# Hybrid diffusion step on one Trainium2 core: where two groups of modulation weights are issued, and how the prologue is ordered

## The chip, the core and the metric

The kernel runs on one core of a Trainium2 chip. The metric is the device time of one execution in microseconds. Engines are named as the profile names them: PE is TensorE (matrix products, with PEld its weight loads), DVE is VectorE, ACT is ScalarE, POOL is GpSimd, and SP is the engine that issues most of the DMA transfers.

## The reference

Two layers (DEPTH = 2, width D = 1024) are applied to 128 context tokens and 512 latent tokens, 640 tokens in all. Each layer has three parallel mixers on one input projection (a two-directional RWKV-7 scan, differential attention, a Hyena long convolution), an output projection and an MLP. Three parts matter here.

Modulation: a vector of 6 x 1024 numbers per token group and layer, which gives shift, scale and gate of the mixer and of the MLP:

```python
mod_ctx = (jax.nn.silu(c_ctx) @ w_mod[l] + b_mod[l])[None, None, :]
...
sh1, sc1, gt1, sh2, sc2, gt2 = jnp.split(mod, 6, axis=-1)
h = _rmsnorm(x, p['g_mix_pre']) * (1.0 + sc1) + sh1
...
x = x + gt1 * _rmsnorm(mix, p['g_mix_post'])
h = _rmsnorm(x, p['g_ffn_pre']) * (1.0 + sc2) + sh2
...
x = x + gt2 * _rmsnorm(f, p['g_ffn_post'])
```

Hyena filters: a small sine network of the position, whose last weight gives two directions per order, normalised and transformed:

```python
h = (h @ p['hy_w3']).reshape(L, HY_ORDER, HY_DIRS, D_C)
h = h * jnp.exp(-t[:, :, None, None] * jnp.abs(p['hy_decay']))
h_fwd, h_bwd = h[:, :, 0], h[:, :, 1]
filt = jnp.concatenate([h_fwd, zeros, h_bwd[:0:-1]], axis=0)
filt = filt * lax.rsqrt(jnp.sum(filt * filt, axis=0, keepdims=True) + 1e-6)
return jnp.fft.rfft(filt, axis=0)
```

RWKV decay and rate, which go through small weights of rank 64 and then through tanh or sigmoid, per direction `d`:

```python
wl = -jax.nn.softplus(-(p['rwkv_w0'][d] + jnp.tanh(uw[d]) @ p['rwkv_w2'][d])) - 0.5
a = jax.nn.sigmoid(p['rwkv_a0'][d] + ua[d] @ p['rwkv_a2'][d])
```

## The kernel before

Tokens are five tiles of 128 (four latent, one context). Feature-major activations are 128 x 640 tiles. Float32 products of large weights are written as three products of a high and a low part, which a helper (`split`, lines 143 to 149) makes from the raw tile. Raw weight tiles of 512 KB go through one pool of three buffers (`wr`), which the modulation weights share.

The stages of the program follow each other: a prologue (modulation group 0 of layer 0, filter networks and filter spectra of both layers, normalisation of the tokens into `act`), and then for each layer the Hyena columns and long convolution with the RWKV columns (`hyena_rwkv_columns`), the operand stage (`rw_operands` with the q/k/v projections of `qkv_columns`), attention, the scan (`rw_scan`), the output projection, and the MLP.

The order of work is written by Python generators. In the operand stage, `rw_operands` is stepped, and on every fifth step one q or k projection is issued. In the scan, `weave` steps about a dozen actors in rounds (inversions, state updates, finishes), and after each round the generator `back` once. `back` is the modulation: one step of `mod_group` (line 275) issues one load of 512 KB on SP's queue and two products of a 128 x 32 weight (the conditioning) with 512 columns of it into one bank, `psmod` (line 293). A group has 16 such steps, then an add of the bias (line 298), for two of three groups a product with gains, four transposes into columns (`pscol`), small copies, and stores of rows. Group 0 (shift and scale of the mixer) is needed at the layer's beginning, group 1 (gate of the mixer, shift of the MLP) and group 2 (scale and gate of the MLP) after the output projection. `mods_late` yields groups 1 and 2, and then, in the first layer, group 0 of the next one; all 48 (first layer) or 32 steps (second) run in the scan.

A planner with a simulated timeline then orders each engine's queue: among instructions that are ready it prefers those that were written first. `issue_after` ties a block's instructions behind a given one of the same engine.

PSUM has eight banks: in the layer's first part two belong to `b1`, four to `b2` (two tiles of two banks) and two to `hz` (one tile of two banks). `hz` serves the transforms of the convolution, and in the operand stage the products of the decay and rate weights (`mm640`, line 585: two halves of 320 columns into the two banks), which one ScalarE instruction of 640 columns reads with its tanh (lines 929 and 933).

In the prologue, `filter_nets` computes the sine networks of both layers, then the rest of the modulation steps and then the loads of the five token tiles (`xl`) are written; `norm_tok` scales each token by its own norm (line 1423) and `norm_feat` transposes, applies group 0's scale and shift, and splits. `hyena_consts` loads the transform's constants on GpSimd's queue after the third token tile. `filter_spectra` makes, for each layer and order, five tiles of both directions, `hft` (line 1215), their squares for the norm, their sum and difference `hpm` (line 1239, ten 128 x 256 instructions), the high and low parts of these, and the transforms.

Of the kernel before, what the change touches and what calls it, by code (L numbers as in the profile page):

```python
# [111 lines left out]
class Net:  # L112
# [47 lines left out]
    def phz(self, nm="hz"):  # L160
        return self.t(self.hz, [P, 2, 512], F32, "hz", nm)

# [193 lines left out]
    def mods_late(self, l, pool, out):  # L356
        rs = []
        yield from self.mod_group(l, 1, pool, rs)
        d1 = self.mod_rows(rs[0], (0, 1))
        S2 = self.mod_shift(self.mod_cols(rs[0])(2), "S2")  # L360
        yield
        yield from self.mod_group(l, 2, pool, rs)
        G2 = self.mod_scale(self.mod_cols(rs[1])(0), V_GFP, "G2", self.vecs[l])
        d2 = self.mod_rows(rs[1], (2, 3))
        out += [d1, S2, G2, d2]
        yield
        if l + 1 < self.nl:
            yield from self.mods(l + 1, pool)
# [552 lines left out]
    def rw_prep(self, l, p, d, w, tw, ua, w2, a2, smask, S, pair, pool, psm):  # L921
# [11 lines left out]
        nc.scalar.activation(self.h2(aa), self.mm640(a2[ds_, fs], ua[ds_]), AF.Tanh, scale=0.5,  # L933
                             bias=self.hb[:, 4 + 2 * d + p:5 + 2 * d + p])
# [46 lines left out]
        for e in range(2):  # L981
# [5 lines left out]
                "pmid": pmid, "pend": pend}  # L987

# [163 lines left out]
    def filter_loads(self, tp, setup, between):  # L1152
# [5 lines left out]
        for l in range(self.nl):  # L1158
            nc.sync.dma_start(self.vecs[l], I["vec"][l])
            hw1 = self.t(tp, [33, 64], F32, "hw1")  # L1160
            nc.sync.dma_start(hw1, I["hy_w1"][l])
            next(between)
            hw2 = self.t(tp, [64, 64], F32, "hw2")
            nc.sync.dma_start(hw2, I["hy_w2"][l])
            out.append({"w": (hw1, hw2), "h": emb})
        next(setup)
        for l, f in enumerate(out):
            hw3 = f["w3"] = self.t(tp, [P, 1024], F32, "hw3")
            nc.gpsimd.memset(hw3[64:], 0.0)
            nc.sync.dma_start(hw3[:64], I["hy_w3"][l])  # L1170
            next(between)
            dec = f["dec"] = self.t(tp, [P, 256], F32, "hdec")
            nc.sync.dma_start(dec, I["hdec"][l])
        return out

    def filter_nets(self, nets, tp):

        nc = self.nc
        for i, b in enumerate((V_B1, V_B2)):
            for l, f in enumerate(nets):  # L1180
                vec = self.vecs[l]
# [20 lines left out]
    def filter_spectra(self, l, f, tp):  # L1202
# [4 lines left out]
        for o in range(2):  # L1207
            fts = []
            acc = None
            for i in range(NT):  # L1210
                ps = self.pb1("psh")
                nc.tensor.matmul(ps, f["h"][:, i * P:(i + 1) * P], f["w3"][:, o * 512:o * 512 + 512],
                                 start=True, stop=True)
# [5 lines left out]
                fts.append(ft)  # L1219
# [7 lines left out]
                if i in (3, 4):  # L1227
# [6 lines left out]
                    nc.vector.tensor_scalar(out=m[:, cc:cc + 2], in0=psn[:, :2], scalar1=1e-6, scalar2=None, op0=ALU.add)  # L1234
            for cs, op in enumerate((ALU.add, ALU.subtract)):
                spl = []
                for i, ft in enumerate(fts):
                    s = self.t(tp, [P, 256], F32, "hpm")
                    nc.vector.tensor_tensor(out=s, in0=ft[:, 0], in1=ft[:, 1], op=op)
                    hh = self.t(tp, [P, 256], F32R, "hph", bufs=10)  # L1240
                    hl = self.t(tp, [P, 256], F32R, "hpl", bufs=10)
                    self.split(hh, hl, s, "a", "v" if i % 2 else "g")
                    spl.append((hh, hl))
                F = self.t(tp, [P, 2, 512], F32, "hF", bufs=1)
                eo = self.phz("psf")
                for par in range(2):
                    tb = self.dftf[par, cs]
                    for ft_ in range(2):
                        for kt in range(2):
                            a = (tb[:, 0, kt, ft_ * P:(ft_ + 1) * P], tb[:, 1, kt, ft_ * P:(ft_ + 1) * P])  # L1250
                            self.mm3(eo[:, par, ft_ * 256:ft_ * 256 + 256], a, spl[par * 2 + kt], kt == 0, kt == 1)
# [9 lines left out]
                self.mm3(ps[:, :256], (self.dftc[:, cs, 0], self.dftc[:, cs, 1]), spl[4], True, True)  # L1261
# [204 lines left out]
    def prologue(self, xsrc, setup):  # L1466
        nc = self.nc
        with ExitStack() as c:
# [7 lines left out]
            self.filter_nets(nets, ph)  # L1476
            for _ in mods:
                pass
            act = self.act_tiles()
            xn = []  # L1480
            for j in range(NT):
# [4 lines left out]
                if j == 2:  # L1486
                    with self.tc.issue_after(self.last_rstd):
                        self.hyena_consts(ph)
                if j == 2:
                    self.norm_feat(xn, 0, 3, self.G1, self.S1, act, pn, True)  # L1490
# [38 lines left out]
    def qkv_columns(self, l, act, pv):  # L1529
# [14 lines left out]
        pss = [x[:, 0], x[:, 1], y[:, 0], y[:, 1], self.phz("psB1")[:, 0]]  # L1544
# [9 lines left out]
    def layer(self, l, act, xsrc, xdst):  # L1554
# [227 lines left out]
```

## Time and profile before

| | us |
|---|---|
| median of 3 runs (lowest, highest) | 2269.79 (2259.91, 2269.84) |
| the profiled execution, its own time | 2268.23 |
| its span, first to last instruction | 2266.5 |
| TensorE busy | 2129.4 |
| VectorE busy | 1458.9 |
| ScalarE busy | 824.1 |
| GpSimd busy | 799.8 |
| mean granted TensorE clock | 0.974 of full |

Busy time of an engine is the union of its instructions' records; matmuls are pipelined, and a busy TensorE is not one at its peak. The granted clock is that of TensorE, as a share of 2.4 GHz; it has two levels, 1.2 and 2.4 GHz, and a value between is the mean over a stretch. DMA share is the mean busy share of the 16 DMA engines. A name such as `psmod<-wr,sc` is output and inputs of an instruction by the program's names, and L293 the line of the kernel. Groups by stretch ("windows") give, for a piece of the span in us, each engine's busy time and in parentheses its instructions.

### The profile page before, as it was taken

The numbers are of one execution on the slowest core, as the hardware profiler recorded it, in microseconds if no ns is written. First come the engines' busy times: TensorE is split into PE (matmuls) and PEld (weight loads), VectorE is DVE, ScalarE is ACT, GpSimd is POOL, SyncE is SP. The second block draws the span as 40 slices with busy tenths as digits, with TensorE's granted clock in tenths as the row PEclk, the third lists the DMA queues.
The fourth block names the chain that finished last, engine by engine and source line by source line (L and its number), as shares of the span: only waits on it lengthen the run. The fifth ranks groups of instructions, "written<-read, shape, count | busy, mean of one in ns | idle before, by whom it ended". The sixth has DMA issues, their size and how long they took to land. (4 is left out here: it accounts for less than half of the span.)

```text
span 2266.5 us, 33997 instructions
## 1 busy us (share of the span) xinstructions
PE 2129.4 (94%) x13236; PEld 1806.3 (80%) x13236; DVE 1458.9 (64%) x2188; ACT 824.1 (36%) x1644; POOL 799.8 (35%) x781
## 2 busy tenths in 40 slices
PE   7899997899999899999999999889999989999998
PEld 2799985666687799898988999656688878989896
DVE  6776658865575764655666575886576584637475
ACT  4442232653342533222324223265344352313131
POOL 3434434541012424342522443464112232524251
PEclk8899998999999899999999999999999999999999
DMA  8244431135405222222254333223510512222233
GB/s 305 77 139 158 132 100 63 57 124 195 162 3 182 75 84 72 87 75 86 76 173 174 105 121 103 72 77 105 196 39 26 205 47 93 76 75 87 81 105 118
DMA packets 86071, 245.42 MB, mean 108 GB/s; under 512 B 12196, under 2 KB 24996, under 8 KB 85909
## 3 DMA queue, kind: packets, MB, share of 16 engines
q1 hardware_dynamic: 80148, 222.34, 29.1%
q0 software_dynamic: 5760, 20.91, 3.0%
q8 instruction: 104, 1.70, 0.3%
q14 instruction: 59, 0.48, 0.1%
HBM read 214.80 MB, written 28.87 MB: 108 GB/s over the span
## 5 line engine op out<-in xcount | busy, mean ns | idle before, releaser
L388 PE MATMUL psA<-act,wh 128*128 128x320 f32 x1472 | 304.2, 319 | 1.1 <-ACT uhr L1503 0.5
L388 PEld LDWEIGHTS psA<-act,wh 128*128 128x128 f32 x1472 | 238.0, 192 | 11.3 <-issue 8.6
L176 PE MATMUL psB<-wl,f 128*128 128x512 f32 x560 | 218.4, 390 | 0.9 <-POOL wl L143 0.9
L177 PE MATMUL psB<-wh,f 128*128 128x512 f32 x560 | 218.4, 390 | 0.0
L143 POOL TENSOR_TENSOR wl<-wr,wh 128x1024 fp32r<-128x1024 f32 x42 | 103.4, 2461 | 304.2 <-DVE wh L149 136.7
L175 PE MATMUL psB<-wh,f 128*128 128x512 f32 x560 | 209.4, 390 | 0.0
L388 PE MATMUL psA<-act,wl 128*128 128x320 f32 x736 | 180.3, 316 | 0.8 <-DVE wl L143 0.8
L143 DVE TENSOR_TENSOR wl<-wr,wh 128x1024 fp32r<-128x1024 f32 x84 | 105.2, 1252 | 63.2 <-ACT wh L147 61.7
L457 POOL TENSOR_TENSOR fft<-ffb 128x512 f32<-128x512 f32 x56 | 89.7, 1601 | 128.3 <-DMA ffb<-in_w_ff_dram 55.4
L388 PEld LDWEIGHTS psA<-act,wl 128*128 128x128 f32 x736 | 127.1, 192 | 3.5 <-issue 2.1
L147 ACT CAST wh<-wr 128x1024 fp32r<-128x1024 f32 x63 | 66.1, 1049 | 168.4 <-PE psB L177 85.6
L176 PEld LDWEIGHTS psB<-wl,f 128*128 128x128 f32 x560 | 105.2, 188 | 22.8 <-POOL wl L143 1.3
L177 PEld LDWEIGHTS psB<-wh,f 128*128 128x128 f32 x560 | 105.2, 188 | 21.8
L175 PEld LDWEIGHTS psB<-wh,f 128*128 128x128 f32 x560 | 105.2, 188 | 21.6
L149 DVE CAST wh<-wr 128x1024 fp32r<-128x1024 f32 x63 | 51.1, 812 | 91.8 <-PE psB L177 63.5
L1054 DVE TENSOR_TENSOR x<-b,cmask 128x512 f16<-128x512 f32 x120 | 80.4, 686 | 33.5 <-PE b L1053 33.2
L147 ACT CAST f<-ffr 128x640 fp32r<-128x640 f32 x64 | 43.8, 726 | 154.3 <-DVE ffr L497 154.3
L1063 ACT CAST t<-px 128x512 f16<-128x512 f32 x100 | 58.7, 588 | 102.0 <-PE px L1058 100.8
L505 DVE TENSOR_TENSOR ffr<-ffr,psF 128x320 f32<-128x320 f32 x140 | 67.4, 482 | 37.2 <-POOL ffr L505 20.6
L505 POOL TENSOR_TENSOR ffr<-ffr 128x320 f32<-128x320 f32 x56 | 54.8, 978 | 95.8 <-DVE ffr L505 84.8
L1025 PE MATMUL b<-ZR,bp 128*128 128x256 f32 x320 | 85.5, 392 | 1.6 <-DVE x L1054 0.8
L177 PE MATMUL psF<-ffS,wl 128*128 128x320 f32 x256 | 80.4, 314 | 5.2 <-DVE wl L143 5.2
(461 smaller groups left out, 6038.1 us busy)
## 6 DMA issues: line engine op xcount, KB each, us to landing
wr<-in_w_mod_dram SPq DMA_DIRECT2D x83, 512.0 KB
wr<-in_w_ff_dram SPq DMA_DIRECT2D x72, 512.0 KB
wr<-in_w_in_dram SPq DMA_DIRECT2D x46, 512.0 KB
x<-x SPq DMA_DIRECT2D x30, 512.0 KB
ffa<-in_w_ff_dram SPq DMA_DIRECT2D x28, 512.0 KB
ffb<-in_w_ff_dram SPq DMA_DIRECT2D x28, 512.0 KB
dft<-in_k_dftf_dram POOLq DMA_DIRECT2D x16, 512.0 KB, 6.7
dft<-in_k_dfti_dram POOLq DMA_DIRECT2D x16, 512.0 KB, 4.9
```

The source lines that it names most:

```text
L143: eng.tensor_tensor(out=l, in0=src, in1=h.bitcast(F32), op=ALU.subtract)
L147: self.nc.scalar.copy(out, in_)
L149: self.nc.vector.tensor_copy(out, in_)
L175: nc.tensor.matmul(out, a[0], b[0], start=first, stop=False)
L176: nc.tensor.matmul(out, a[0], b[1], start=False, stop=False)
L177: nc.tensor.matmul(out, a[1], b[0], start=False, stop=last)
L388: self.nc.tensor.matmul(ps[:, hf, :320], (h, l)[a][:, k * P:(k + 1) * P], act[b][k][:, hf * 320:hf * 320 + 320], start=k == 0 and i == 0, ...
L457: sub = lambda o, x, y: nc.gpsimd.tensor_tensor(out=o, in0=x, in1=y, op=ALU.subtract)
L505: add = lambda o, a, b, e=nc.vector, op=ALU.add: e.tensor_tensor(out=o, in0=a, in1=b, op=op)
L1025: nc.tensor.matmul(ps[:, 2 * e:2 * e + 2], bp[:, q, e], s["ZR"][:, :, j], start=True, stop=True)
L1054: nc.vector.tensor_tensor(out=vw(x16), in0=vw(ps), in1=cm(i), op=ALU.mult)
L1063: nc.scalar.copy(t16, ps1)
```

## The change

Five edits, in the order of the code of a run:

- In the prologue, eleven modulation steps are issued with the five token tiles among them (from the third step of these on, one on every second), each tile loaded and scaled by its own norm. Only then come the filter networks of layer 0, the rest of the modulation and `norm_feat`. The constants of the transform and the filter networks of layer 1 come after `norm_feat`.
- The two filter directions are added and subtracted on the last weight of the network, 64 rows, by GpSimd, so `hft` holds sum and difference at once. The `hpm` instructions go, and splits take 512 columns instead of 256. At the first tap, where the backward direction counts as zero, half of the sum of both parts is written to both. The norm is halved to match. `hft` has two buffers instead of six.
- The operand stage opens PSUM pools of its own: `b2` as before, and in place of the two-bank `hz` one bank `h1` and one bank `pm`.
- The products of the decay and rate weights are read in halves of 320 columns, each through the one bank `h1` (`tanh640`).
- `mods_late` (groups 1 and 2) is stepped in the operand stage, once per step of `rw_operands`, before attention. The scan steps only group 0 of the next layer, and in the last layer nothing.

```diff
@@ mods_late
         out += [d1, S2, G2, d2]
         yield
-        if l + 1 < self.nl:
-            yield from self.mods(l + 1, pool)
@@ rw_prep
-        nc.scalar.activation(self.h2(sw), self.mm640(w2[ds_, fs], tw[ds_]), AF.Tanh, scale=0.5,
-                             bias=self.hb[:, 2 * d + p:2 * d + p + 1])
+        self.tanh640(sw, w2[ds_, fs], tw[ds_], 2 * d + p)
...
+    def tanh640(self, out, lhsT, rhs, i):
+        for hf in range(2):
+            sl = slice(hf * 320, hf * 320 + 320)
+            ps = self.ph1("ps640")[:, :320]
+            self.nc.tensor.matmul(ps, lhsT, rhs[:, sl], start=True, stop=True)
+            self.nc.scalar.activation(out[:, sl], ps, AF.Tanh, scale=0.5, bias=self.hb[:, i:i + 1])
@@ filter_loads
+            w3 = f["w3"] = self.t(tp, [P, 2, 512], F32, "hws")
+            nc.gpsimd.memset(w3[64:], 0.0)
+            for q, op in enumerate((ALU.add, ALU.subtract)):
+                nc.gpsimd.tensor_tensor(out=w3[:64, :, q * 256:q * 256 + 256], in0=hw3[:64, :, :256], in1=hw3[:64, :, 256:],
+                                        op=op)
@@ filter_spectra
-                ft = self.t(tp, [P, 2, 256], F32, "hft", bufs=6)
+                ft = self.t(tp, [P, 2, 256], F32, "hft", bufs=2)
...
                 if i in (0, 4):
-                    nc.vector.memset(ft[0:1, 1], 0.0)
+                    tap = self.t(tp, [1, 1, 256], F32, "htap", bufs=1)
+                    nc.vector.tensor_tensor(out=tap, in0=ft[0:1, 0:1], in1=ft[0:1, 1:2], op=ALU.add)
+                    nc.vector.tensor_scalar(out=ft[0:1], in0=tap.to_broadcast([1, 2, 256]), scalar1=0.5, scalar2=None,
+                                            op0=ALU.mult)
...
-            for cs, op in enumerate((ALU.add, ALU.subtract)):
-                spl = []
-                for i, ft in enumerate(fts):
-                    s = self.t(tp, [P, 256], F32, "hpm")
-                    nc.vector.tensor_tensor(out=s, in0=ft[:, 0], in1=ft[:, 1], op=op)
-                    hh = self.t(tp, [P, 256], F32R, "hph", bufs=10)
-                    hl = self.t(tp, [P, 256], F32R, "hpl", bufs=10)
-                    self.split(hh, hl, s, "a", "v" if i % 2 else "g")
-                    spl.append((hh, hl))
+                hh = self.t(tp, [P, 2, 256], F32R, "hph", bufs=6)
+                hl = self.t(tp, [P, 2, 256], F32R, "hpl", bufs=6)
+                self.split(hh, hl, ft, "a", "v" if i % 2 else "g")
+                spl.append((hh, hl))
+            for cs in range(2):
+                sp = [(x[:, cs], y[:, cs]) for x, y in spl]
@@ prologue
-            self.filter_nets(nets, ph)
-            for _ in mods:
-                pass
-            act = self.act_tiles()
             xn = []
-            for j in range(NT):
+
+            def tokens(j):
                 x = self.t(px, [P, D], F32, "xl")
                 nc.sync.dma_start(x, xsrc[j])
                 self.norm_tok(x, x, pn, self.t(px, [P, D], F16, "xj", bufs=1))
                 xn.append(x)
...
+            for n in range(11):
+                next(mods)
+                if n >= 2 and n % 2 == 0:
+                    tokens(n // 2 - 1)
+            self.filter_nets(nets[:1], ph)
+            for _ in mods:
+                pass
+            act = self.act_tiles()
+            self.norm_feat(xn, 0, 3, self.G1, self.S1, act, pn, True)
             self.norm_feat(xn, 3, 5, self.G1, self.S1, act, pn, True)
             with self.tc.issue_after(self.last_rstd):
+                self.hyena_consts(ph)
                 next(setup)
+            self.filter_nets(nets[1:], ph)
@@ layer
-            self.psum(c1, b2=2, hz=1)
             with ExitStack() as ch:
+                self.psum(ch, b2=2, hz=1)
                 ur = self.hyena_rwkv_columns(l, act, pR, self.sb(ch, "hx", 1), ch)
+            self.psum(c1, b2=2, h1=1, pm=1)
+            self.pmtag = "pm"
...
+            back = self.mods_late(l, self.pS, late)
             next(cols)
             for n, _ in enumerate(self.rw_operands(l, ur, (pk, prw), (ptmp, psm))):
                 if n % 5 == 4:
                     next(cols, None)
+                next(back, None)
+            for _ in back:
+                pass
...
-            self.rw_scan(l, prs, prg, self.sb(c, "rf", 1), self.mods_late(l, self.pS, late))
+            self.rw_scan(l, prs, prg, self.sb(c, "rf", 1), iter(()) if last else self.mods(l + 1, self.pS))
```

## Rows read from the trace of the kernel before

**Rows 1.** Page, part 1: busy us, share of the span, instructions.
```profile
PE 2129.4 (94%) x13236; PEld 1806.3 (80%) x13236; DVE 1458.9 (64%) x2188; ACT 824.1 (36%) x1644; POOL 799.8 (35%) x781
```

**Rows 2.** Stretches, prologue: length, busy us (instructions) by engine, granted clock, DMA share, GB/s.
```profile
30.00:40.00 10.00, 6.87 (x37) 3.01 (x38) 7.33 (x10) 6.56 (x14) 6.80 (x9) 0.86 1.03 406
40.00:90.00 50.00, 38.25 (x169) 29.09 (x170) 38.25 (x80) 27.81 (x61) 20.34 (x27) 0.69 0.42 141
```

**Rows 3.** Timeline, TensorE: start us, length us, engine, line, operation, operands, count.
```profile
41.67 1.06 PE L170 MATMUL pscol<-ident,mrow 128*128 128x128 f32 x4
...
85.68 1.52 PE L388 MATMUL psA<-act,wh 128*128 128x320 f32 x2
```

**Rows 4.** Stretches, all engines: operand stages and scans of both layers.
```profile
283.00:388.80 105.80, 90.91 (x475) 76.17 (x474) 74.56 (x92) 31.51 (x54) 40.36 (x28) 0.90 0.23 72
...
487.60:692.00 204.40, 198.92 (x1736) 142.21 (x1736) 122.44 (x241) 79.57 (x170) 35.65 (x39) 0.99 0.41 135
...
1370.00:1472.50 102.50, 93.81 (x522) 80.76 (x520) 74.25 (x93) 31.80 (x54) 42.77 (x32) 0.95 0.25 82
...
1569.80:1756.00 186.20, 181.54 (x1669) 138.09 (x1669) 118.60 (x234) 79.76 (x170) 37.55 (x39) 1.00 0.31 102
```

**Rows 5.** Stretches, tails of both operand stages.
```profile
360.00:370.00 10.00, 2.19 (x6) 1.34 (x6) 9.96 (x11) 0.00 (x0) 3.30 (x3) 0.57 0.19 52
370.00:380.00 10.00, 8.71 (x25) 6.34 (x24) 9.50 (x12) 0.85 (x2) 5.53 (x3) 0.57 0.01 2
1445.00:1455.00 10.00, 3.23 (x15) 2.24 (x14) 10.00 (x13) 0.37 (x1) 4.90 (x4) 0.77 0.09 23
1455.00:1465.00 10.00, 9.32 (x31) 7.41 (x32) 9.96 (x13) 0.00 (x0) 5.51 (x3) 0.72 0.10 30
```

**Rows 6.** Stretches, modulation products and adds alone (columns PE, PEld, DVE), both scans.
```profile
487.60:692.00 204.40, 45.73 (x192) 6.77 (x192) 2.07 (x3) 0.99 0.41 135
1569.80:1756.00 186.20, 31.39 (x128) 4.45 (x128) 1.38 (x2) 1.00 0.31 102
```

**Rows 7.** Stretches, second scan: early, and after modulation has ended.
```profile
1570.00:1603.00 33.00, 32.59 (x250) 16.62 (x249) 16.74 (x26) 14.15 (x31) 6.47 (x10) 1.00 0.77 255
1660.00:1700.00 40.00, 40.00 (x418) 36.37 (x415) 30.55 (x62) 20.43 (x43) 7.85 (x7) 1.00 0.01 3
```

**Rows 8.** Stretch, modulation products alone, second scan, early.
```profile
1570.00:1603.00 33.00, 15.67 (x64) 2.18 (x64) 0.00 (x0) 1.00 0.77 255
```

**Rows 9.** Timeline, second scan, all engines.
```profile
1576.88 0.39 PE L1053 MATMUL b<-t,m 128*128 128x128 f16 x4
...
1577.20 1.05 PE L293 MATMUL psmod<-wr,sc 128*32 128x512 f32 x4
...
1577.31 0.69 DVE L1054 TENSOR_TENSOR x<-b,cmask 128x512 f16<-128x512 f32 x1 [0.48 <-PE b L1053]
...
1578.18 0.40 PE L1058 MATMUL px<-x,tt 128*128 128x128 f16 x4
...
1578.42 0.39 PE L1060 MATMUL px<-tt,x 128*128 128x128 f16 x4
```

**Rows 10.** Tile sw, ScalarE's read of a tanh product: ns min/median/max.
```profile
L929 ACT ACTIVATE sw<-ps,hb x4: 786/794/797, 297.3 to 336.7; 128x640 f32<-128x640 f32 x4
```

**Rows 11.** Timeline, VectorE, prologue.
```profile
38.25 0.68 DVE L298 TENSOR_TENSOR mrow<-psmod,mbias 128x512 f32<-128x512 f32 x1
...
57.44 1.88 DVE L1423 TENSOR_SCALAR xl<-xl,rstd 128x1024 f32<-128x1024 f32 x2
```

**Rows 12.** VectorE by group, 0 to 86 us: busy us, mean ns, idle before.
```profile
L1239 DVE TENSOR_TENSOR hpm<-hft 128x256 f32<-128x256 f32 x14 | 8.5, 621 | 0.3
...
L143 DVE TENSOR_TENSOR hpl<-hpm,hph 128x256 fp32r<-128x256 f32 x6 | 5.0, 842 | 1.4 <-ACT hph L147 1.4
...
L1184 DVE TENSOR_SCALAR ha<-ps,vec 64x640 f32<-64x640 f32 x4 | 3.7, 930 | 1.0 <-PE ps L585 1.0
...
L1147 DVE SCALAR_TENSOR_TENSOR ha<-hq,ha 64x640 f32<-64x640 f32 x4 | 3.3, 816 | 0.1
```

More of the change, by code (lines that the diff above doesn't have):

```diff
@@ L161, in phz, with ph1 @@
         return self.t(self.hz, [P, 2, 512], F32, "hz", nm)
+    def ph1(self, nm="h1"):
+        return self.t(self.h1, [P, 512], F32, "h1", nm)
     def pb1(self, nm="b1"):
@@ L928, in rw_prep @@
         sw, aa = S("sw"), S("aa")
-        nc.scalar.activation(self.h2(sw), self.mm640(w2[ds_, fs], tw[ds_]), AF.Tanh, scale=0.5,
-                             bias=self.hb[:, 2 * d + p:2 * d + p + 1])
+        self.tanh640(sw, w2[ds_, fs], tw[ds_], 2 * d + p)
         yield
         nc.vector.tensor_scalar(out=sw, in0=sw, scalar1=0.5, scalar2=0.5, op0=ALU.mult, op1=ALU.add)
-        nc.scalar.activation(self.h2(aa), self.mm640(a2[ds_, fs], ua[ds_]), AF.Tanh, scale=0.5,
-                             bias=self.hb[:, 4 + 2 * d + p:5 + 2 * d + p])
+        self.tanh640(aa, a2[ds_, fs], ua[ds_], 4 + 2 * d + p)
         yield
@@ L1164, in filter_loads @@
             nc.sync.dma_start(hw2, I["hy_w2"][l])
-            out.append({"w": (hw1, hw2), "h": emb})
+            out.append({"l": l, "w": (hw1, hw2), "h": emb})
         next(setup)
         for l, f in enumerate(out):
-            hw3 = f["w3"] = self.t(tp, [P, 1024], F32, "hw3")
+            hw3 = self.t(tp, [P, 2, 512], F32, "hw3", bufs=1)
             nc.gpsimd.memset(hw3[64:], 0.0)
-            nc.sync.dma_start(hw3[:64], I["hy_w3"][l])
+            nc.sync.dma_start(hw3[:64], I["hy_w3"][l].rearrange("p (o c) -> p o c", o=2))
             next(between)
+            w3 = f["w3"] = self.t(tp, [P, 2, 512], F32, "hws")
[3 more added lines that the diff above has]
+                                        op=op)
             dec = f["dec"] = self.t(tp, [P, 256], F32, "hdec")
@@ L1179, in filter_nets @@
         for i, b in enumerate((V_B1, V_B2)):
-            for l, f in enumerate(nets):
-                vec = self.vecs[l]
+            for f in nets:
+                vec = self.vecs[f["l"]]
                 ps = self.mm640(f["w"][i], f["h"], 64)
@@ L1207, in filter_spectra @@
         for o in range(2):
-            fts = []
+            spl = []
             acc = None
@@ L1211, in filter_spectra @@
                 ps = self.pb1("psh")
-                nc.tensor.matmul(ps, f["h"][:, i * P:(i + 1) * P], f["w3"][:, o * 512:o * 512 + 512],
-                                 start=True, stop=True)
-                ft = self.t(tp, [P, 2, 256], F32, "hft", bufs=6)
+                nc.tensor.matmul(ps, f["h"][:, i * P:(i + 1) * P], f["w3"][:, o], start=True, stop=True)
+                ft = self.t(tp, [P, 2, 256], F32, "hft", bufs=2)
                 nc.vector.tensor_tensor(out=ft, in0=ps.rearrange("p (d c) -> p d c", d=2),
@@ L1233, in filter_spectra @@
                     cc = (i == 4) * 4 + o * 2
-                    nc.vector.tensor_scalar(out=m[:, cc:cc + 2], in0=psn[:, :2], scalar1=1e-6, scalar2=None, op0=ALU.add)
-            for cs, op in enumerate((ALU.add, ALU.subtract)):
-                spl = []
-                for i, ft in enumerate(fts):
-                    s = self.t(tp, [P, 256], F32, "hpm")
-                    nc.vector.tensor_tensor(out=s, in0=ft[:, 0], in1=ft[:, 1], op=op)
-                    hh = self.t(tp, [P, 256], F32R, "hph", bufs=10)
-                    hl = self.t(tp, [P, 256], F32R, "hpl", bufs=10)
-                    self.split(hh, hl, s, "a", "v" if i % 2 else "g")
-                    spl.append((hh, hl))
+                    nc.vector.tensor_scalar(out=m[:, cc:cc + 2], in0=psn[:, :2], scalar1=0.5, scalar2=1e-6,
+                                            op0=ALU.mult, op1=ALU.add)
+                hh = self.t(tp, [P, 2, 256], F32R, "hph", bufs=6)
[4 more added lines that the diff above has]
+                sp = [(x[:, cs], y[:, cs]) for x, y in spl]
                 F = self.t(tp, [P, 2, 512], F32, "hF", bufs=1)
@@ L1543, in qkv_columns @@
         x, y = self.pb2("psB"), self.pb2("psB")
[L1544 removed]
+        pss = [x[:, 0], x[:, 1], y[:, 0], y[:, 1], self.ph1("psB1")]
         self.denseB(pss, [I["w_v"][l, i] for i in range(4)], act)
```

10 lines of the change are left out of this document (2 added, 8 removed).

## The prediction, made before the change ran

> **What bounds the kernel now.** I read the page first: TensorE is busy for 94% of the span, VectorE for 64% [rows 1]. Next I read stretches of ten to fifty microseconds, to see where TensorE still has room, because only there can moved work be free. It has room in two places that the change touches. In the prologue, from 40 to 90 us, TensorE is busy 38.25 of 50 us at a mean granted clock of 0.69 [rows 2]: 11.75 us idle, and about 0.31 x 38.25 = 11.9 us given to its half rate of 1.2 GHz, together 23.6 us. The end of this stretch is the first projection of the input, which starts at 85.68 us [rows 3]. The second place is the operand stage of each layer (from the end of the long convolution to the first attention scores): 105.80 us with TensorE busy 90.91 in the first layer, 102.50 with 93.81 in the second [rows 4], so 14.9 and 8.7 us idle, nearly all near the end, where VectorE is busy 9.5 to 10 of every 10 us and the clock falls to 0.57 and 0.72 [rows 5]. In the scans there is hardly room: 198.92 of 204.40 and 181.54 of 186.20 us [rows 4]. The modulation products are 45.73 us of the first (48 steps) and 31.39 us of the second (32 steps) [rows 6]. A step is one 512 KB load and two matmuls of 128x32 weights by 512 columns; that is 0.95 and 0.98 us of TensorE.
>
> **The change, part by part.** All terms are against the profiled execution: span 2266.5 us, its own time 2268.2, that is 1.6 us under the median of the three runs (2269.8).
>
> *Scan, what leaves.* Groups 1 and 2 of a layer, 32 steps, leave its scan; in the first layer group 0 of the next layer (16 steps) now comes from the start, in the second nothing is left. Where many inversions are in flight, TensorE is full without modulation: 40.00 of 40 us from 1660 us on [rows 7]. There a step that leaves gives its time back. The two scans agree: the first has 16 steps more and is 204.40 - 186.20 = 18.2 us longer [rows 4], 1.14 us a step. So the first layer gives 32 x 0.95 = 30.5 us, and the second layer's later 16 steps give 16 x 0.98 = 15.7 us. Its first 16 are another matter. From 1570 to 1603 us they take 15.67 us of 33 [rows 7, 8], but they fill waits: at 1577.20 a step runs while VectorE multiplies (1577.31 to 1578.00), and the matmul that needs the product starts at 1578.18 [rows 9]. Without the step that matmul would start at the same moment. Between nothing and 15.7 us I take 5. Sum: **-51 us**. Ends: -62 (all 64 steps at their full time), -35 (a quarter of the 46.2 lost to waits that come up, and nothing from the first 16).
>
> *Operand stage, what arrives.* The same 64 steps, 32 x 0.95 + 32 x 0.98 = 62 us of TensorE. They are issued one per step of the operand generator, in the first 34 of its some 54 steps, between the q/k projections. What can hide them is the 14.9 + 8.7 = 23.6 us of idle time and about 8 us of half rate in the tails [rows 4, 5] (8.71 us at 0.57 and 9.32 us at 0.72 are 3.7 and 2.6, the small rows the rest), 32 us in all. But that room lies at the end, when VectorE holds the stage, and the steps are issued early, where TensorE is full of projections. They help only so far as projections and value products slide into the tail. I take 17 of the 32, so **+45 us**; ends +30 and +62. Each step also brings its load on SP's queue, past q/k stores, the loads back of q and k, and the w_in and w_v loads, and it shares the three raw-weight buffers with these. 16.8 MB more over 105 us is 160 GB/s on top of 72 and 82 [rows 4], far below the 406 GB/s that the queues reach [rows 2], so I cost the transfers at nothing; if a w_v tile waits behind them for a buffer, its products are what is late next, and they have the tail to be late in. Per group there are also two memsets on GpSimd, six 4 KB loads, two VectorE passes (2.07 us for three [rows 6], so 0.69 each), four transposes, small column copies and two row stores: about 3 us of VectorE per layer, moved from a stage where it has room to one whose end it holds. If they fall into its gaps early, nothing; at the end 6 us for both layers. I take **+1**.
>
> *Tanh products in halves.* The two-bank tile shared by both halves becomes a one-bank tile with one buffer: 16 products, each with a second matmul that now waits until ScalarE has read the first half. A read of 640 columns takes 0.79 us [rows 10], half of it some 0.45 plus the signal. What stands behind that matmul on TensorE is a projection or a modulation step. If the order puts such work between the halves the wait costs nothing, else 16 x 0.75 = 12 us. Before, consecutive products waited for that read too. I take **+2**.
>
> *Prologue.* Before, w_mod lands, then its add on VectorE waits until 38.25, the column transposes run at 41.67, and the last two token tiles are normalised only at 57.44 [rows 3, 11]. Now the five token tiles are loaded among the last weights. The bytes are the same and the queues are full (share 1.03 [rows 2]), so the last weight lands about when the last token did, but the tokens are then already normalised. VectorE loses, before the first projection, 14 combinations of 0.62 us [rows 12], 8.5 us, plus half of the filter nets (the four passes of 0.93 and 0.82 us [rows 12] and their like, 8 us of 16), which move behind the token tiles; splits of 512 columns replace twice as many of 256 (0.84 each with their waits [rows 12]). Added: two passes over one row where a memset of it stood, eight times in all, each bounded by the 256-column pass of 0.62 us, and four weight combinations on GpSimd, which idles there. The spectra's constants are loaded later; projections, which could start near 62 us, cover that. About 10 us of filter products then remain that are done by 85.68 today, so of 24 us of earlier start half is a gain: **-14 us**, within 0 (the normalisation stays bound by VectorE and ScalarE) and -22 (nearly all of the 23.6 us).
>
> Sum: -51 + 45 + 1 + 2 - 14 = -17 us. 2268.2 - 17 = 2251, and with the 1.6 us to the median **2252 us**.
>
> One rule of the Trainium skill speaks against the move. Ahead of a modulation step the trace shows 0.32 us between the starts of the two groups, where two ordinary ones follow in 0.24 [rows 9]. "TensorEngine Tiling (Array Packing)", section "Tiling Modes", says that a change of tiling mode drains TensorE. In the scan such a drain can fall into a wait; among back-to-back projections each of the 64 steps would pay it on both sides, as an estimate 64 x 0.16 = 10 us, and the sum would be 2262. The row prices only one side, so I leave the sum.
>
> **Rivals.**
> 1. *The operand stage absorbs nearly all.* For it: 32 us of room [rows 4, 5], and a full TensorE no longer falls to half rate. Against: the issue order. Growth +30, scans -62, prologue -20: 2268 - 49 = about 2220.
> 2. *Only the prologue's start moves, not its end.* For it: VectorE is busy 38.25 of 50 us there [rows 2] and the normalisation itself needs it. Prologue 0, the rest -3: about 2266.
> 3. *Slower: modulation was a filler in the scan and is a load in the operand stage.* Place: the operand generator, whose products for VectorE's chain stand behind one step each. For it: the chain passes through TensorE a dozen times and VectorE, full in the tail [rows 5], starts later by each wait, so no room is gained. Price: +62, +6, +10 for the halves; the scans give only -35; prologue -10: 2268 + 33 = about 2300. It decides from the point where the stages grow by more than the scans shrink plus the prologue's gain.
> 4. *The clock.* TensorE's clock fell to 0.57 where it was busy 2.19 of 10 us [rows 5]; without steps the second layer's first 33 us hold 17 us of products [rows 7, 8]. At half rate these cost up to 17 us: 2268. "TensorE: Matmul & The Clock Gate", section "HAM oscillation — how this bites in real kernels", says that gaps in a kernel's matmul work bring the slow clock back; the tails agree. In this scan's first microseconds the clock is 1.00, with the steps in it.
>
> **How the numbers follow.** Forecast (2236 to 2264) 0.42, rival 1 0.17, rival 2 0.14, rival 3 0.20, rival 4 0.07. About 0.5%, or 11 us, is what a measurement of this kernel can tell from no change. Faster by more (below 2258.4): 0.32 of the forecast, rival 1, and 0.05 of the others, 0.54. Within: 0.10 of the forecast, most of rivals 2 and 4, and the mild end of rival 3, 0.28. Slower: 0.18. The range 2216 to 2286 leaves out the worst half of rival 3 and the tip of rival 1; the forecast's own range is 2236 to 2264.
>
> **What would show it.** First projection near 62 us instead of 85.68; first attention scores later after the convolution's end, by 15 to 30 us per layer, with the tail's clock near 1.00; no modulation products in the second scan, which then takes about 165 us from last value product to first output product, and the first about 174. If the stages grow by 60 us, or the scans shrink by less than 35, or the first projection stays near 85, the prediction is wrong in that term.

## The result and the profile after

The changed kernel takes 2301.32 us (median of 4 runs, 2295.5 to 2303.96) against 2268.89 (2259.91 to 2269.84): ratio 1.0148, 95% interval 1.0115 to 1.0182. It is slower. 2252 was forecast, with a range up to 2286. Its profiled execution has a span of 2302.2 us, 35.7 more than before.

On the page [rows 1] TensorE is busy 14 us longer than before and VectorE 25 us less:

```profile
PE 2143.0 (93%) x13236; PEld 1814.1 (79%) x13236; DVE 1433.7 (62%) x2148; ACT 826.4 (36%) x1640; POOL 812.2 (35%) x775
```

So of the 35.7 us, 13.6 are busy time of TensorE and 22.1 idle time. The stretches of the changed kernel that answer to [rows 2] and [rows 4] (prologue, operand stage and scan of the first layer, then of the second):

```profile
40.00:90.00 50.00, 37.94 (x210) 29.47 (x211) 37.90 (x75) 28.32 (x56) 25.16 (x23) 0.81 0.43 150
275.60:434.90 159.30, 131.98 (x639) 93.95 (x639) 75.87 (x104) 35.78 (x65) 47.04 (x38) 0.86 0.43 145
530.20:701.00 170.80, 166.82 (x1604) 136.19 (x1603) 118.17 (x233) 79.56 (x170) 34.36 (x36) 0.99 0.21 64
1374.50:1533.10 158.60, 138.61 (x682) 96.73 (x681) 76.96 (x105) 35.53 (x63) 44.30 (x36) 0.87 0.45 153
1629.20:1788.20 159.00, 150.74 (x1536) 133.51 (x1536) 114.91 (x226) 79.58 (x170) 36.76 (x37) 1.00 0.05 16
```

The reader is to see two things. In the scans the two groups of modulation are gone and the time with them (the first scan still holds group 0 of the next layer). In both operand stages TensorE is idle for 27 and 20 us and its mean clock is 0.86 and 0.87, where [rows 4] has 0.90 and 0.95. Cut at first and last starts of one tile's products, the whole span is:

| stretch | before | after | |
|---|---|---|---|
| start to first projection | 85.7 | 87.5 | +1.8 |
| to the convolution's last transform, layer 1 | 195.9 | 188.1 | -7.8 |
| operand stage 1, to first scores | 107.2 | 159.3 | +52.1 |
| attention 1, to last value product | 98.4 | 95.3 | -3.1 |
| scan 1, to first output product | 204.9 | 170.8 | -34.1 |
| output product, MLP | 508.6 | 506.0 | -2.6 |
| first projections and convolution, layer 2 | 167.7 | 167.5 | -0.2 |
| operand stage 2 | 104.1 | 158.6 | +54.5 |
| attention 2 | 97.0 | 96.1 | -0.9 |
| scan 2 | 186.5 | 159.0 | -27.5 |
| to the end | 510.5 | 514.0 | +3.5 |

The operand stages give 106.6 us away, the scans win 61.6. Where the 106.6 us lie, the same two stages of the kernel before and then the modulation products alone in the changed one tell (length, busy us of TensorE first):

```profile
281.60:388.80 107.20, 92.31 (x485) 77.57 (x485) 75.93 (x94) 31.51 (x54) 41.76 (x32) 0.90 0.22 71
1368.40:1472.50 104.10, 95.42 (x533) 82.36 (x532) 75.78 (x96) 31.80 (x54) 42.77 (x32) 0.95 0.24 80
```

```profile
275.60:434.90 159.30, 24.86 (x108) 3.84 (x108) 1.37 (x2) 0.86 0.43 145
1374.50:1533.10 158.60, 27.35 (x112) 3.95 (x112) 1.35 (x2) 0.87 0.45 153
```

TensorE's idle time grows by 23.7 us. Its busy time grows by 82.9: 52.2 are modulation products, and 30.7 other work, at the lower clock and with 83 more instructions of it between the two marks. TensorE's timeline in the first operand stage shows how (start, length, operation, count of instructions, idle time before it and what ended it; four instructions of `psmod` are one step):

```profile
276.17 1.91 PE L296 MATMUL psmod<-wr,sc 128*32 128x512 f32 x12
281.75 1.92 PE L296 MATMUL psmod<-wr,sc 128*32 128x512 f32 x4 [3.67 <-DMA wr<-in_w_mod_dram]
...
348.31 1.05 PE L296 MATMUL psmod<-wr,sc 128*32 128x512 f32 x4
...
368.31 1.91 PE L296 MATMUL psmod<-wr,sc 128*32 128x512 f32 x12
...
377.02 1.44 PE L389 MATMUL psA<-act,wh 128*128 128x320 f32 x4 [4.25 <-DVE wh L149]
...
388.06 1.91 PE L296 MATMUL psmod<-wr,sc 128*32 128x512 f32 x12
393.58 1.55 PE L296 MATMUL psmod<-wr,sc 128*32 128x512 f32 x4 [3.62 <-DMA wr<-in_w_mod_dram]
397.59 1.44 PE L389 MATMUL psA<-act,wh 128*128 128x320 f32 x4 [2.46 <-ACT wh L147]
```

Three steps run in one clump (x12), one for each raw buffer; then TensorE stands 3.7 us until the next modulation tile has landed, or 4.2 and 2.5 us until a projection's weight is split. After the wait that ends at 281.75 a step takes 1.92 us, at a granted clock of 0.50; at 348.31 one takes 1.05, at 1.00. The three steps of 276.17, also at 1.00, take 1.91 us together and not three times 1.05: steps that stand next to each other overlap. What SP's queue shows of the same waits, from 250 to 434 us (instruction that waits, line that it waits for: us in total, times, longest):

```profile
SPq L190 <- PE psmod L296: 29.6, 5, 10.5
SPq L291 <- PE psmod L296: 22.8, 12, 5.8
SPq L291 <- DVE wl L143: 16.7, 4, 7.2
```

L190 loads projection and value weights, L291 modulation. A projection's load stands for up to 10.5 us in SP's queue for a buffer that a `psmod` product has yet to free. The loads of raw tiles on SP's queue from 240 to 460 us are shown below (count, ns, first and last start), first before, then after. The last projection weight goes out at 391.3 us instead of 288.5, and the value weights follow:

```profile
L187 SPq DMA_DIRECT2D wr<-in_w_in_dram x5: 327/333/382, 243.6 to 288.5; - x5
L187 SPq DMA_DIRECT2D wr<-in_w_v_dram x4: 327/330/333, 299.3 to 333.7; - x4
```

```profile
L291 SPq DMA_DIRECT2D wr<-in_w_mod_dram x30: 327/328/1235, 246.7 to 389.8; - x30
L190 SPq DMA_DIRECT2D wr<-in_w_in_dram x7: 328/328/421, 250.0 to 391.3; - x7
L190 SPq DMA_DIRECT2D wr<-in_w_v_dram x4: 327/354/376, 391.7 to 402.3; - x4
```

From 246.7 to 402.3 us these are 41 loads, 3.8 us each on the average.

### The profile page after: what moved, and what is told of

It is laid out like the page before. It is cut to its first block, busy times and chain, and to the rows that moved or that the text cites. A ratio compares the mean times of both kernels' runs of the same rounds, so it can differ in the third digit from the quotient of the medians.

```text
span 2302.2 us, 33952 instructions
## 1 busy us (share of the span) xinstructions
PE 2143.0 (93%) x13236; PEld 1814.1 (79%) x13236; DVE 1433.7 (62%) x2148; ACT 826.4 (36%) x1640; POOL 812.2 (35%) x775
## 4 chain that ended last, share of the span: by engine, by line
PE 43%; DVE 7%; DMA 3%; POOL 2%; issue 2%; ACT 2%; SPq 0%; DVEq 0%; POOLq 0%; ACTq 0%
PE psB L179 5%; PE psB L178 5%; PE psB L180 5%; PE psA L389 5%; PE psF L180 3%; PE psF L179 3%; PE psF L178 3%; PE b L1032 1%; PE psmod L296 1%; PE pss L683 1%; DMA wr<-in_w_mod_dram 1%; DMA ffb<-in_w_ff_dram 1%; DVE wl L143 1%; PE psD L178 1%; PE psD L180 1%
## 5 line engine op out<-in xcount | busy, mean ns | idle before, releaser
L389 PEld LDWEIGHTS psA<-act,wh 128*128 128x128 f32 x1472 | 246.2, 199 | 39.7 <-DVE wh L149 13.2
L389 PE MATMUL psA<-act,wl 128*128 128x320 f32 x736 | 186.2, 325 | 3.0 <-DVE wl L143 3.0
L1061 DVE TENSOR_TENSOR x<-b,cmask 128x512 f16<-128x512 f32 x120 | 79.9, 684 | 18.1 <-PE b L1060 17.6
L296 PE MATMUL psmod<-wr,sc 128*32 128x512 f32 x332 | 78.9, 697 | 12.5 <-DMA wr<-in_w_mod_dram 11.5
```

The lines of the kernel that those rows point to most:

```text
L296: nc.tensor.matmul(ps[32 * j:32 * j + 32], self.sc[:, k], w[:, jj], start=k == 0, stop=k == KD - 1)
L389: self.nc.tensor.matmul(ps[:, hf, :320], (h, l)[a][:, k * P:(k + 1) * P], act[b][k][:, hf * 320:hf * 320 + 320], start=k == 0 and i == 0, ...
L1061: nc.vector.tensor_tensor(out=vw(x16), in0=vw(ps), in1=cm(i), op=ALU.mult)
```

## The experiments

The expectations count growth from the first projection to the first scores, 98.6 us for both layers: the 106.6 above less the 7.8 and 0.2 by which the convolutions got shorter. Below, "stages" are the two operand stages alone (107.2 and 104.1 before). Intervals are of the ratio to before.

### Which part costs

**e1_mods_back.**

```diff
+        if l + 1 < self.nl:
+            yield from self.mods(l + 1, pool)
...
-            back = self.mods_late(l, self.pS, late)
...
-                next(back, None)
...
-            self.rw_scan(l, prs, prg, self.sb(c, "rf", 1), iter(()) if last else self.mods(l + 1, self.pS))
+            self.rw_scan(l, prs, prg, self.sb(c, "rf", 1), self.mods_late(l, self.pS, late))
```

> The changed kernel with groups 1 and 2 stepped in the scan again, as before; the new prologue, the combined filter weight, the one-bank tanh halves stay. Measured so far: from the first input projection to the first attention scores the two layers take 303.1 and 271.8 us before and 347.4 and 326.1 after, together 98.6 us more. Theory A (the move alone makes the kernel slower): these stretches come back to within 5 us of 303 and 272, the time is 2258 to 2270. Rival B (the halves through one bank, or the prologue, carry a part of the loss): a stretch stays 10 us or more above before, or the first projection's later stages lose, and the time is 2278 or more.

2283.97 us, 1.0036 to 1.0085; stages 119.1 and 110.2. Rival B: moving the modulation cost 17 us, and 15 were still missing, with both stages longer without any modulation in them. ScalarE's reads of the tanh halves in this run (start, length, idle before):

```profile
295.13 0.52 ACT L996 ACTIVATE sw<-ps,hb 128x320 f32<-128x320 f32 x1
...
302.81 0.53 ACT L996 ACTIVATE sw<-ps,hb 128x320 f32<-128x320 f32 x1 [0.32 <-PE ps L995]
...
307.02 0.53 ACT L996 ACTIVATE sw<-ps,hb 128x320 f32<-128x320 f32 x1 [1.72 <-PE ps L995]
...
311.28 0.53 ACT L996 ACTIVATE sw<-ps,hb 128x320 f32<-128x320 f32 x1 [1.83 <-PE ps L995]
...
315.65 0.53 ACT L996 ACTIVATE aa<-ps,hb 128x320 f32<-128x320 f32 x1 [1.30 <-PE ps L995]
320.09 0.53 ACT L996 ACTIVATE aa<-ps,hb 128x320 f32<-128x320 f32 x1 [3.92 <-PE ps L995]
...
324.53 0.53 ACT L996 ACTIVATE aa<-ps,hb 128x320 f32<-128x320 f32 x1 [2.08 <-PE ps L995]
...
329.63 0.51 ACT L996 ACTIVATE aa<-ps,hb 128x320 f32<-128x320 f32 x1
```

Before, four reads of 640 columns served the same products:

```profile
297.27 0.79 ACT L929 ACTIVATE sw<-ps,hb 128x640 f32<-128x640 f32 x1
305.15 0.79 ACT L929 ACTIVATE sw<-ps,hb 128x640 f32<-128x640 f32 x1 [7.09 <-PE ps L585]
...
310.19 0.80 ACT L933 ACTIVATE aa<-ps,hb 128x640 f32<-128x640 f32 x1 [1.62 <-PE ps L585]
...
315.33 0.80 ACT L933 ACTIVATE aa<-ps,hb 128x640 f32<-128x640 f32 x1 [2.37 <-PE ps L585]
```

Each half waits for the bank, and its product then for its turn among the projections: some 4.3 us from one read to the next and eight reads, where there were four. (The layer's other eight, from 345.26 us on, follow each other in 1.4 to 3.8 us.) VectorE, which needs both halves, starts later, at 311.84 instead of 306.39, after 7.53 us idle:

```profile
311.84 0.49 DVE L934 TENSOR_SCALAR sw<-sw 128x640 f32<-128x640 f32 x1 [7.53 <-ACT sw L996]
...
321.45 0.69 DVE L149 CAST wh<-wr 128x1024 fp32r<-128x1024 f32 x1 [6.46 <-PE psA L391]
```

**e5_two_banks** puts the two-bank tile back as well (`hz=1` and `mm640`, as before).

> The run with the modulation back in the scan, and the two-bank tanh product of before put back too: what is left of the change is the prologue's order and the combined filter weight. With the halves, that run was 2284 against 2269 before, and its two operand stretches (last transform of the convolution to first attention scores) were 11.9 and 6.1 us longer. Theory H (the halves through one bank cost these 18 us: each half waits for the bank and then for its turn in TensorE's queue): both stretches return to within 3 us of before, the time is 2262 to 2269. Rival P (the loss comes from elsewhere in the new prologue or PSUM pools): the time stays at 2276 or more.

2266.94 us, 0.9981 to 1.0012; stages 107.2 and 104.4. Theory H: the halves cost 17.0 us. And prologue and filter weight together give 3 us in the medians, which the interval does not tell from nothing.

**e6_halves_two_shared_banks.**

```diff
-            ps = self.ph1("ps640")[:, :320]
+            ps = self.pb1("ps640")[:, :320]
```

> The run with the modulation back in the scan, the tanh halves kept but through the two one-bank buffers of b1 that other small products of the stage use, not through the single bank h1. Theory H1 (it is the single bank that makes a half wait for the half before it): the stretches fall back most of the way, time 2266 to 2275. Rival H2 (it is twice the number of ScalarE reads and TensorE turns, whatever the bank): the time stays at 2280 or more.

2272.2 us, 1.0000 to 1.0025. Theory H1: 12 of the 17 us are the single bank.

**e12_change_shared_banks**: the same edit in the changed kernel.

> The changed kernel with one edit: the tanh halves go through the two buffers of b1. Theory H1 (the single bank's turn costs 12 of 17 us, whatever else stands in the stage): time 2285 to 2293. Rival (behind the waits for loads the halves cost nothing): 2298 or more.

2289.71 us, 1.0065 to 1.0115: 11.6 us less than the changed kernel, as 11.8 were without the modulation steps: the two losses add up.

### What of the modulation costs

**e3_no_mod_loads** (no `dma_start` for groups 1 and 2):

```diff
-                    nc.tensor.matmul(ps[32 * j:32 * j + 32], self.sc[:, k], w[:, jj], ...)
+                    src = w[:, jj] if g == 0 else self.mact[jj][k].bitcast(F32)[:, :512]
+                    nc.tensor.matmul(ps[32 * j:32 * j + 32], self.sc[:, k], src, ...)
```

> The changed kernel without the 64 loads of groups 1 and 2: their products keep number, shape and place but read a resident activation tile, so the modulation values are not computed. Theory R (the loads, through the three raw buffers and SP's queue, hold up the projections' weights): of the 98.6 us that the two stretches grew, at most the products' own 62 us stay, less what their idle time absorbs: growth 30 to 62, time 2230 to 2265. Rival Q (what hurts is where the products stand in TensorE's queue, ahead of the operand chain): growth stays above 85 us, time 2288 to 2301.

2239.78 us, 0.9850 to 0.9902; stages 125.6 and 129.9. Theory R, clearly: all products are still computed, and 61.5 us are gone. They did not keep their place, though. The modulation products in the two stages of this run, to be read against the same rows of the changed kernel above, and two of its clumps:

```profile
275.60:401.20 125.60, 13.79 (x88) 2.86 (x88) 1.38 (x2) 0.93 0.21 68
1343.20:1473.10 129.90, 16.54 (x100) 3.23 (x100) 1.38 (x2) 0.96 0.23 73
```

```profile
248.20 4.50 PE L300 MATMUL psmod<-act,sc 128*32 128x512 f32 x40
...
316.52 3.63 PE L300 MATMUL psmod<-act,sc 128*32 128x512 f32 x28
```

Where no step waits for a tile to land, up to ten stand in a row and overlap, 0.45 us each, and 17 of the 64 run ahead of the stages. All 64 take 39.5 us of TensorE here (30.3 of them in the stages) and 59.6 in the changed kernel. So the loads cost 61.5 us with what they do to the products.

**e4_short_mod_products** (`n = 512 if g == 0 or k == 0 else 16` columns).

> The changed kernel with all loads of groups 1 and 2, but 56 of their 64 steps multiply only 16 of 512 columns, so most of the modulation is not computed; some 62 us of TensorE shrink to about 16. Theory R (loads and buffers set the pace): the two stretches still grow by 50 us or more over before, time 2253 to 2285. Rival Q (place in TensorE's queue): growth falls to 15 or less, time 2205 to 2225.

2283.69 us, 1.0041 to 1.0082; stages 141.4 and 158.4. Theory R: with hardly any products but all loads, 17.6 us are gained over the changed kernel.

**e5_small_mod_loads** (`dma_start(w[:, :, :16], ...[:, :, :16])`, products as in the run without loads, and for each a short one of 16 columns that reads the loaded tile and so frees it: 12.8 us of TensorE in all).

> The changed kernel with each load of groups 1 and 2 cut from 512 KB to 16 KB, into the same three buffers and by the same queue; the products read a resident tile, with one more product of 16 columns on the loaded tile that frees its buffer (the modulation is not computed). TensorE gets about 10 us more work. Theory R1 (what costs is the turn of three buffers and SP's order: a weight load stands behind a modulation load whose buffer a queued product has yet to free): growth stays above 75 us, time 2278 to 2312. Theory R2 (what costs is the transfer time of 33.6 MB): growth falls to that of the run without loads plus 10, time 2240 to 2275.

2281.09 us, 1.0036 to 1.0080; stages 148.0 and 149.6. Theory R1: with a thirty-second of the bytes 20 of 61.5 us come back. The short products hide a part of what the bytes cost, at most their 12.8 us, so the bytes' part is some 20 to 33 us: not all of the loss, but not nothing.

**e7_own_three_buffers** and **e8_own_twelve_buffers** (the same loads of 16 KB and the same products, `w = self.t(self.pwm, [P, 2, 16], F32, "wm")`, with 3 and 12 buffers):

> The run with modulation loads of 16 KB (2281 us), the same loads now in three buffers of their own instead of the three raw-weight buffers; still on SP's queue in the same order, products as there, and the modulation is not computed. Theory B (sharing the raw buffers holds up the projections' weights): growth of the two stretches falls from 80 us to 50 or less, time 2240 to 2255. Rival S (the order of SP's queue does: a weight load stands behind a modulation load that waits for its buffer): growth stays above 65, time 2265 to 2283.

> As the run with three buffers of its own, with twelve. Theory B: hardly different from three, 2235 to 2255. Rival S: with twelve a modulation load seldom waits for a buffer, so SP's queue is free and the loss goes only here: 2240 to 2255, 15 us or more below the run with three.

2269.35 us (0.9985 to 1.0016; stages 136.2 and 142.8) and 2251.09 us (0.9900 to 0.9942; 124.4 and 134.4). By the times rival S came true in both runs (the growth with three, 64 us, just misses its 65). But sharing counts too: own buffers give 11.7 us, and nine buffers more another 18.3. From 250 to 434 us SP stands 32.8 us behind `psmod` products with three buffers and 3.6 with twelve. The 11.3 us by which the run with twelve is still above the run without loads are no more than the short products' 12.8. With twelve, the value weights leave SP's queue (240 to 460 us) 15 us after those of the kernel before, not 69:

```profile
L190 SPq DMA_DIRECT2D wr<-in_w_in_dram x5: 327/333/602, 248.1 to 312.3; - x5
L190 SPq DMA_DIRECT2D wr<-in_w_v_dram x4: 328/342/426, 312.9 to 349.1; - x4
```

### How many steps, and where

**e10_one_group_early**, **e9_one_group_late** and **e11_both_groups_late** step `back` from the first or the 35th step of the stage on, halves through the shared banks. With one group the other runs in the scan; with both, the steps that are left follow right behind the operand steps:

```diff
+            grp = 0
...
-                next(back, None)
+                if n >= 34 and grp < 17:     # n >= 0 in the early run; no bound on grp for both groups
+                    grp += 1
+                    next(back)
...
-            self.rw_scan(l, prs, prg, self.sb(c, "rf", 1), iter(()) if last else self.mods(l + 1, self.pS))
+            self.rw_scan(l, prs, prg, self.sb(c, "rf", 1), back)     # not with both groups
```

> Halves through the two shared banks (2272 with all modulation in the scan), and only group 1, 16 steps a layer, in the operand stage, from the 35th of its steps on, when the q and k projections are all written; group 2 runs in the scan. Theory L (the loss is the modulation loads standing ahead of the projections' weights): there is nothing behind them but the four value weights, the steps fill TensorE's idle tail, a stretch grows by 8 us or less, the scans give 13 to 16 us each: 2250 to 2260. Rival V (the value weights are held up in the same way): a stretch grows by 20 us or more, time 2278 or more.

> The same 16 steps a layer, but from the first step of the operand stage on, as in the changed kernel. Theory L: they stand among the projections and cost about half of what the 32 do (54 us of load loss), time 2275 to 2295, 20 us or more above the late run. Rival N (only the number of steps counts, not the place): within 8 us of the late run.

> Both groups, 32 steps a layer, from the 35th step of the operand stage on, halves through the two shared banks. Theory L: the scans give 59 us as in the changed kernel; the tail has room for some 16 steps, the others come after the value products or hold them up: growth 30 to 45 us a layer less than in the changed kernel cannot be had in full; time 2250 to 2278, below the changed kernel's 2301 by 23 us or more. Rival V: 2285 or more.

Late: 2276.46 us (1.0023 to 1.0048); early: 2254.37 (0.9909 to 0.9955); both late: 2319.05 (1.0193 to 1.0243). My theory L fell: late is 22 us worse than early. The late products of layer 1, and below them the first scores of the attention stage:

```profile
L296 PE MATMUL psmod<-wr,sc x64: 592/617/1062, 328.1 to 407.0; 128*32 128x512 f32 x64
```

```profile
L685 PE MATMUL pss<-kr,qp x64: 592/594/1222, 386.7 to 484.7; 128*128 128x512 f32 x64
```

They run 20 us into attention, whose two stages are 17.2 and 11.9 us longer than before (both groups: 51.0 and 48.7). Rival V doesn't hold either: the value weights go out by 347 us, and operand stage 1 is 108.6 us; only stage 2 grew, to 121.1. Early, one group is done in time. Its loads:

```profile
L291 SPq DMA_DIRECT2D wr<-in_w_mod_dram x14: 327/330/1227, 248.2 to 304.6; - x14
L190 SPq DMA_DIRECT2D wr<-in_w_in_dram x7: 327/383/873, 251.4 to 323.7; - x7
L190 SPq DMA_DIRECT2D wr<-in_w_v_dram x4: 333/345/371, 324.3 to 351.6; - x4
```

These 25 loads, 4.1 us each on the average, have gone out 43 us before the first scores (394.6); the 41 of the changed kernel need 156 us, where the stage before had 107. The first 16 steps a layer lengthen the stages by 16.6 us against the run with all in the scan (236.6 instead of 220.0), the second 16 by another 72 (308.5, **e12_change_shared_banks**), while either 16 take some 31 us from the two scans. That the second 16 find no room for their products isn't the reason: without loads, the products of all 32 lengthen the stages by 26 us.

**e15_one_group_spread** (`if n % 2 == 0 and grp < 17`):

> One group in the operand stage, from its first step on, but one step on every second of the generator's steps, so that two or three loads stand between two projections and not five. Theory S (a projection's weight load waits for the modulation loads ahead of it to find a buffer): fewer per projection are hidden better, 2243 to 2252, against 2254 for one on every step. Rival E (the group's end counts: the later it ends the more it reaches into the value weights): 2256 to 2270.

2252.96 us, 0.9898 to 0.9951: in neither theory's range, and not told apart from the early run.

### The prologue

**e13_order_only** and **e14_filter_only** are the kernel before with one of the two edits of the prologue.

> The kernel before with the new order of the prologue alone (tokens among the modulation weights, networks of layer 1 behind the normalisation); filter directions, halves and modulation as before. Forecast for prologue and filter together was -14 us, measured -2 to -3 against before. Theory D (the bytes of the tokens stand ahead of the last modulation weights, so the bias add comes 11 us later and takes back what the earlier normalisation gives): within 4 us of before, 2265 to 2273. Rival F (the order gains and the filter part loses): 2256 to 2263.

> The kernel before with the directions combined on the filter weight alone, the prologue in its old order. Theory D: VectorE has 6 to 8 us less to do before the projections take TensorE over, but the first projection waits for the normalisation: 0 to -4 us, 2265 to 2270. Rival F: it loses what the order gains, 2274 or more.

2263.72 us (0.9954 to 0.9983) and 2264.19 us (0.9956 to 0.9987): each alone gives 6 to 7 us, which neither theory had, and together (**e5_two_banks**) they give 3 in the medians. The normalisation's transposes (first and last start) with the order alone, the filter weight alone, and both:

```profile
L170 PE MATMUL pstr<-ident,xl x40: 272/320/473, 50.3 to 74.9; 128*128 128x128 f32 x40
```

```profile
L173 PE MATMUL pstr<-ident,xl x40: 270/328/477, 44.5 to 73.7; 128*128 128x128 f32 x40
```

```profile
L173 PE MATMUL pstr<-ident,xl x40: 270/273/476, 50.2 to 78.5; 128*128 128x128 f32 x40
```

Either edit lets them end 8 to 9 us earlier than before (82.8); with both only 4. Why was not tried. **e16_group_spread_filter_only** takes the order out of the spread run:

> The run with one group spread over every second step (2253), with the prologue back in its old order and the combined filter weight kept. Theory D2 (each of the two prologue edits gives 6 to 7 us alone and they take each other's place, so that together they give only 1 to 3): this is 3 to 5 us faster than with both, 2247 to 2251. Rival (the prologue's parts don't matter once the operand stage holds a group): 2252 to 2256.

2245.78 us, 0.9880 to 0.9916: 7.2 us less than with both in the medians (2245.0 to 2251.4 against 2250.7 to 2254.1), more than the 3 to 5 that theory D2 had. So here, too, the order takes away what the filter weight gives; by what path stays open. This kernel beats the one before by 23 us and the changed one by 55.

## Why the prediction was wrong, point by point

- **Scan, -51.** Right in kind, measured -61.6, the end of the range that I gave for all steps at their full time. The early steps of the second layer did not merely fill waits: that scan fell by 27.5 us, of 31.39 us of modulation in it [rows 6]. Rival 4 did not come.
- **Products in the operand stage, +45.** Without loads the stages grow by 44.2 us, 18.0 of which the run with the modulation back shows without any steps. So the products cost 26, below my range. But the reason is not the one that I gave, idle room that hides them: I carried the 62 us over from the scans, where steps run one at a time, and without loads the 64 steps take 39.5 us, 30.3 of them in the stages, since steps in a row overlap. Of these 30.3 the stages hide about 4. The 10 us that I set beside the sum for changes of the tiling mode are separated from this by no run.
- **"I cost the transfers at nothing": the step that failed.** I divided bytes by rate (160 GB/s against 406). The loads cost 61.5 us. The bytes are some 20 to 33 of it, as an estimate from the run with small loads. 30.0 more, with small loads, go with buffers of their own and with nine more of them. So what I left out is the turn of three shared buffers: load, stand behind the products queued on TensorE, free, and SP's queue stands meanwhile with the projections' loads in it. I named the queue and the buffers and stopped there. The trace before had a bound: in the first scan the 48 modulation loads go out from 480.6 to 611.0 us through the same three buffers, 2.8 us each. At that pace 41 loads are 114 us in a stage of 107, with nothing yet for the longer use of a projection's tile; measured were 156.
- **Halves, +2 (0 to 12).** They cost 17.0 us, 11.8 of them by the single bank. I priced one ScalarE read; the price is a turn of the bank, some 4.3 us in the first half of the stage, on the way to VectorE, which holds the stage's end.
- **Prologue, -14.** Together about -3. The first projection came at 87.47 us, not near 62. The modulation's add moved from 38.25 to 49.54 [rows 11], behind the tokens' loads, and products of the spectra then run among the transposes. That is not the whole cause: with the order alone the add is as late, at 48.6 us, and the first projection comes at 81.7; with the filter weight alone it comes at 79.0. What the two do to each other stays open. In its time rival 2 was right for this stretch.
- **Tail clock near 1.00.** Wrong: 0.73 from 370 to 400 us, among the waits shown above; over the whole span it is 0.963, and 0.979 without the loads. "TensorE: Matmul & The Clock Gate" of the Trainium skill, section "HAM oscillation — how this bites in real kernels", names gaps in the matmul work as what brings the slow clock back; the stages' 0.86 and 0.87 agree.

With the measured terms: -61.6 + 26 + 61.5 + 17 - 3 = +40, against 32 measured and 35.7 between the profiles; attention's -4 is in none of the terms, and the terms mix stretches of a profile with whole times. Rival 3 gave the time, about 2300, but by luck: it had 62 us of products in front of VectorE's chain, and the run without loads computes them all and is 29 us faster than the kernel before.

## What to carry to other kernels

Before moving loads into another stage, count them and not only their bytes: loads times the turn of a buffer (landing, use, release) over the number of buffers, against the stage's length. Here 25 loads fitted and cost little; with 41, the loads delayed the weights behind them in the same queue. (Two counts are no proof of the formula; it is an estimate to make first.) A product's price also depends on its neighbours: the 128x32 steps took 1.05 us one at a time and 0.45 in a row of ten. When a product that feeds the bounding engine loses its second bank, price a full turn in TensorE's queue for each piece. Two edits that give 7 us each alone may give 3 together, so each is to be run alone.
